# A gather, cumulative sum and projection on one core: another prologue, and GpSimd's drain moved into its own stream

## The chip, the cores and the metric

One core of a Trainium2 chip. The metric is the device time of one execution in microseconds (us); single executions of one kernel on an undisturbed chip lay within about 1% of each other. Where a ratio of two kernels is given, it is the mean time of the one's fast runs over the mean of the other's fast runs of the same rounds, so not quite the ratio of the medians that are quoted beside it. Brackets hold the 95% interval.

## The reference

```python
B, S, N, D = (16, 4096, 2048, 512)
# x [B, S, D] float32; indices [B, N] int64, sorted rows without repeats; w [D, D] float32
gathered = x[b_idx, indices, :].copy()
cs = np.cumsum(gathered, axis=1)
return np.matmul(cs, w).astype(np.float32)
```

## The kernel before

256 tiles of 128 gathered rows go through in pairs, called groups below: 128 groups. GpSimd gathers a tile (256 KB), ACT casts a pair to float16, PE sums along the rows with a triangular matrix, VectorE adds the carry, PE projects with w, ACT copies the result from PSUM, SP stores 512 KB. Every engine has a hand-written stream, in which `need(sem, n)` waits.

```python
ctx.enter_context(tc.tile_critical(no_gpsimd_drain=False))     # line 78: closes with a drain of all engines
...
def gather(t):                              # GpSimd
    g, r = divmod(t, R)                     # R = 2
    pool.need(s_c, g + 1 - NG // R)         # NG = 16: the buffer is free
    if t < FIRST:
        pool.need(s_first, 16)              # the small index load idx_first has landed
    ...
def cast(g):                                # ACT, one pair
    ...
def drain(g):                               # ACT: PSUM to an output buffer (not GpSimd's drain)
    act.need(s_o[g % NO], 16 * (g // NO))   # NO = 8 output buffers
    act.need(s_b, R * (g + 1))
    nc.scalar.copy(out=ob[g % NO][:], in_=pb[g % NB][:]).then_inc(s_e, 1)
def store(g):                               # SP
    sp.need(s_e, g + 1)
    nc.sync.dma_start(out=dst, in_=ob[g % NO][:]).then_inc(s_o[g % NO], 16)
...
# SP: idx_first, two index loads, then all of w, then the stores
# ACT:
cast(0)
act.need(s_w, 16)
nc.scalar.copy(out=w16[:], in_=w32[:]).then_inc(s_wc, 1)
for g in range(1, AH + 1):                  # AH = 2
    cast(g)
for g in range(G):
    if g + AH + 1 < G:
        cast(g + AH + 1)
    drain(g)                                # so store g follows the cast of group g + 3
```

## Time and profile before

The lines that carry the argument stand in the prediction. In short:

| kernel before, profiled run | |
|---|---|
| time | 357.12 us, median of 3 (356.56 to 357.59); the profiled run took 356.41, its span is 354.6 |
| first and last gather issued | 3.25 and 322.66 us |
| last gather landed | 337.49 us |
| first store issued, last store landed | 20.71 and 348.27 us |
| from the last store's landing to the end | 6.33 us, of which 4.97 GpSimd's drain |
| DMA share and rate, 31 to 323.6 us | 1.03, 413 GB/s |

It is to be read as a start (until DMA is full), a long middle in which DMA is full (share 1.03) and the gathers fall behind (8.6 us under way at 60 to 100 us, 15.1 at 310 to 340), a tail after the last gather, and a closing part.

### The profile page before, as it was taken

The page shows a single profiled execution, that of the slowest core. Times are in us where ns is not written, and L with a number is a line of the kernel's source. Part 1 is how long each engine was busy: PE and PEld are TensorE (multiplying, and loading weights), DVE is VectorE, ACT ScalarE, POOL GpSimd, SP SyncE. Part 2 cuts the span into 40 slices and gives each one's busy share as a digit, 9 for nine tenths or more (in the row PEclk, how much of TensorE's full clock was granted, in tenths as well). Part 3 has the DMA queues.
Part 4 walks back from the last instruction along what each step waited for, and adds up shares of the span by engine and source line. Part 5 has one row for each costly group of instructions (what it writes and reads, how often), then busy time and mean ns, then how long its engine had stood idle before and what let it go on. Part 6 is the DMA issues. An engine that isn't in the chain of part 4 may idle for free.

```text
span 354.6 us, 5833 instructions
## 1 busy us (share of the span) xinstructions
PE 301.8 (85%) x2050; PEld 149.2 (42%) x2050; DVE 178.1 (50%) x260; ACT 257.9 (73%) x258; POOL 243.7 (69%) x264
## 2 busy tenths in 40 slices
PE   0497799999899999899898988989989889898880
PEld 0253354444354444444444444444444444444440
DVE  1354465555555555555554554645555555555530
ACT  0776687787788787777777777877878778687760
POOL 6777777777777777777777777777777777774000
PEclk9999999999999999999999999999999999999995
DMA  6789999999999999999999999999999999999761
GB/s 222 224 241 384 409 410 401 415 411 418 412 417 416 415 414 415 413 416 416 415 415 414 414 413 413 411 417 415 413 417 413 416 413 414 412 415 414 293 244 74
DMA packets 40029, 135.92 MB, mean 383 GB/s; under 512 B 6465, under 2 KB 6721, under 8 KB 40001
## 3 DMA queue, kind: packets, MB, share of 16 engines
q0 software_dynamic: 20480, 67.13, 48.5%
q1 hardware_dynamic: 19520, 68.43, 47.8%
q8 instruction: 17, 0.28, 0.3%
q14 instruction: 12, 0.09, 0.1%
HBM read 68.42 MB, written 67.11 MB: 382 GB/s over the span
## 4 chain that ended last, share of the span: by engine, by line
POOL 50%; DMA 22%; issue 17%; PE 5%; ACT 3%; ACTq 0%; SPq 0%
POOL g L108 50%; DMA g<-in_x_dram,idxg 21%; PE pb L160 4%; ACT g L120 3%; PE pa L128 1%; ACT ob L172 1%; DMA idx_first<-in_indices_dram 1%; ACTq L23 0%; SPq L284 0%; SPq L78 0%
## 5 line engine op out<-in xcount | busy, mean ns | idle before, releaser
L108 POOL DMA_INDIRECT g<-in_x_dram,idxg x254 | 240.5, 947 | 77.4 <-issue 71.3
L160 PE MATMUL pb<-w,cst 128*128 128x512 f16 x1024 | 263.5, 381 | 0.0
L148 DVE TENSOR_TENSOR cst<-pa,cst 128x512 f16<-128x512 f32 x240 | 166.0, 692 | 138.1 <-PE pa L128 137.3
L120 ACT CAST g<-g 128x1024 f16<-128x1024 f32 x128 | 133.6, 1045 | 66.9 <-issue 32.2
L172 ACT COPY ob<-pb 128x1024 f32<-128x1024 f32 x128 | 129.2, 1010 | 11.4 <-PE pb L160 9.8
L128 PE MATMUL pa<-ut,g 128*128 128x128 f16 x1024 | 101.1, 222 | 38.5 <-ACT g L120 37.8
L128 PEld LDWEIGHTS pa<-ut,g 128*128 128x128 f16 x1024 | 69.4, 99 | 128.4 <-ACT g L120 97.6
L160 PEld LDWEIGHTS pb<-w,cst 128*128 128x128 f16 x1024 | 90.0, 98 | 62.0 <-issue 1.1
L143 DVE CAST cst<-pa 128x512 f16<-128x512 f32 x16 | 11.1, 692 | 20.4 <-PE pa L128 20.4
L120 ACT ACT_TABLE_LOAD x1 | 1.3, 1283 | 9.5 <-DMA g<-in_x_dram,idx_first 9.5
L229 PE MATMUL pb<-ident,idxf 128*128 128x128 f32 x2 | 0.9, 462 | 4.2 <-DVE idxf L225 4.2
L108 POOL DMA_INDIRECT g<-in_x_dram,idx_first x2 | 2.1, 1043 | 1.6 <-DMA idx_first<-in_indices_dram 1.3
L225 DVE CAST idxf<-idx 128x128 f32<-128x128 uint32 x2 | 0.5, 226 | 4.1 <-DMA idx<-in_indices_dram 4.1
L229 PEld LDWEIGHTS pb<-ident,idxf 128*128 128x128 f32 x2 | 0.4, 182 | 4.4 <-issue 4.2
L252 ACT CAST w<-w 128x2048 f16<-128x2048 f32 x1 | 1.9, 1892 | 0.0
L234 DVE CAST idxg<-pb 128x128 uint32<-128x128 f32 x2 | 0.6, 292 | 0.3
L198 POOL MEMSET ident<- 128x128 f32 x1 | 0.2, 205 | 0.5 <-SPq L78 0.5
L201 POOL TENSOR_SCALAR_AFFINE_SELECT ident<-ident 128x128 f32<-128x128 f32 x1 | 0.3, 288 | 0.1
L273 POOL MEMSET const-float32-0.0<- 128x1 f32 x1 | 0.1, 100 | 0.3 <-issue 0.3
L210 POOL TENSOR_SCALAR_AFFINE_SELECT ut<-ut 128x128 f16<-128x128 f16 x1 | 0.3, 292 | 0.0
L199 POOL MEMSET ut<- 128x128 f16 x1 | 0.2, 206 | 0.0
L273 POOL MEMSET const-uint8-127<- 128x1 uint8 x1 | 0.1, 117 | 0.0
(2 smaller groups left out, 0.2 us busy)
## 6 DMA issues: line engine op xcount, KB each, us to landing
out_dram<-ob SPq DMA_DIRECT2D x128, 512.0 KB, 7.2
g<-in_x_dram,idxg POOLq DMA_INDIRECT x254, 10.2
w<-in_w_dram SPq DMA_DIRECT2D x1, 1024.0 KB, 5.6
idx<-in_indices_dram SPq DMA_DIRECT2D x2, 128.0 KB, 2.3
g<-in_x_dram,idx_first POOLq DMA_INDIRECT x2, 5.1
idx_first<-in_indices_dram SPq DMA_DIRECT2D x1, 2.0 KB, 1.9
```

The costliest lines, as they stand in the source:

```text
L108: nc.gpsimd.indirect_dma_start(out=g32[g % (NG // R)][:, r, :], out_offset=None, in_=x_flat, in_offset=bass.IndirectOffsetOnAxis(ap=ap, ax ...
L120: nc.scalar.copy(out=g16[g % NH][:], in_=g32[g % (NG // R)][:]).then_inc(s_c, 1)
L128: mm = nc.tensor.matmul(out=pa[t % NA][:, c], lhsT=g16[g % NH][:, r, c * P : (c + 1) * P], rhs=ut[:], start=(c == 0), stop=(c == DC - 1),)
L143: nc.vector.tensor_copy(out=dst, in_=pa[t % NA][:]).then_inc(s_d, 1)
L148: nc.vector.tensor_tensor(out=dst, in0=pa[t % NA][:], in1=last.unsqueeze(2).broadcast_to([P, DC, R, Q]), op=mybir.AluOpType.add,).then_inc ...
L160: mm = nc.tensor.matmul(out=pb[g % NB][:, j], lhsT=cst[g % NC][:, c, j, :], rhs=w16[:, c, :], start=(c == 0), stop=(c == DC - 1),)
L172: nc.scalar.copy(out=ob[g % NO][:], in_=pb[g % NB][:]).then_inc(s_e, 1)
L201: nc.gpsimd.affine_select(out=ident[:], in_=ident[:], compare_op=mybir.AluOpType.is_equal, fill=0.0, base=0, pattern=[[-1, P]], channel_mu ...
L225: nc.vector.tensor_copy(out=idxf[:, k, :], in_=idx64[:, k, 0::2]).then_inc(s_if, 1)
L229: nc.tensor.transpose(out=pb[k % NB][:, 0, :P], in_=idxf[:, k, :], identity=ident[:]).then_inc(s_pt, 1)
L234: nc.vector.tensor_copy(out=idxg[:, k, :], in_=pb[k % NB][:, 0, :P]).then_inc(s_prep, 1)
L252: nc.scalar.copy(out=w16[:], in_=w32[:]).then_inc(s_wc, 1)
```

## The change

The intent: w arrives and is cast before the first gather lands (four loads on ACT's own queue, two casts on ACT, two on VectorE); ACT's function table (1.28 us, at 9.45 us in the kernel before) is loaded by a dummy activation while nothing else is there to do; dummy matmuls keep PE busy ahead of the projections, the first of which took 631 ns in the kernel before, and 379 later; the first pair is cast tile by tile; GpSimd's drain, which closed the program, goes behind its last gather.

```diff
+    zeros = const.tile([P, D], FP16)
+    spare = const.tile([P, 1], FP16)
     g32 = [const.tile([P, R, D], FP32, name=f"g32_{i}") for i in range(NG // R)]
...
-    ctx.enter_context(tc.tile_critical(no_gpsimd_drain=False))
+    ctx.enter_context(tc.tile_critical(no_gpsimd_drain=True))
...
+    def cast_first(t):
+        act.need(s_g[t], 16)
+        nc.scalar.copy(out=g16[0][:, t], in_=g32[0][:, t]).then_inc(s_c0, 1)
...
-    nc.sync.dma_start(out=w32[:], in_=w.rearrange("(c p) d -> p c d", p=P)).then_inc(s_w, 16)
...
     for t in range(T):
         gather(t)
+    nc.gpsimd.drain()
+    def busy(n):
+        pe.need(s_z, 1)
+        for _ in range(n):
+            nc.tensor.matmul(
+                out=pb[NB - 1][:, R - 1], lhsT=zeros[:, :P], rhs=zeros[:], start=True, stop=True
+            )
+    nc.vector.memset(zeros[:], 0.0).then_inc(s_z, 1)
...
+    busy(6)          # ahead of the index transposes
...
+    busy(18)         # behind them
...
+    for c in range(DC // 2, DC):
+        dve.need(s_w[c], 16)
+        nc.vector.tensor_copy(out=w16[:, c, :], in_=w32[:, c, :]).then_inc(s_wc, 1)
...
-    cast(0)
-    act.need(s_w, 16)
-    nc.scalar.copy(out=w16[:], in_=w32[:]).then_inc(s_wc, 1)
+    for c in range(DC):
+        nc.scalar.dma_start(out=w32[:, c, :], in_=w[c * P : (c + 1) * P, :]).then_inc(s_w[c], 16)
+    act.need(s_z, 1)
+    nc.scalar.copy(out=spare[:], in_=zeros[:, :1])
+    for c in range(DC // 2):
+        act.need(s_w[c], 16)
+        nc.scalar.copy(out=w16[:, c, :], in_=w32[:, c, :]).then_inc(s_wc, 1)
+    for t in range(R):
+        cast_first(t)
```

(Cut: the semaphores and the wait counts that follow from these lines.)

More of the change, by code (lines that the diff above doesn't have):

```diff
@@ L76 @@
     pb = [ps.tile([P, R, D], FP32, name=f"pb{i}") for i in range(NB)]
-    ctx.enter_context(tc.tile_critical(no_gpsimd_drain=False))
+    ctx.enter_context(tc.tile_critical(no_gpsimd_drain=True))
     def sem(name):
         return tc.alloc_semaphore(name)
-    s_first, s_w, s_ut, s_wc, s_if, s_pt, s_prep = (
-        sem(f"s_{n}") for n in ("first", "w", "ut", "wc", "if", "pt", "prep")
+    s_first, s_z, s_ut, s_wc, s_if, s_pt, s_prep, s_c0 = (
+        sem(f"s_{n}") for n in ("first", "z", "ut", "wc", "if", "pt", "prep", "c0")
     )
+    s_w = [sem(f"s_w{c}") for c in range(DC)]
     s_idx = [sem(f"s_idx{k}") for k in range(KI)]
@@ L100, in gather @@
         g, r = divmod(t, R)
-        pool.need(s_c, g + 1 - NG // R)
+        pool.need(s_c, g - NG // R)
+        if g >= NG // R:
+            pool.need(s_c0, R)
         if t < FIRST:
@@ L120, in cast @@
         nc.scalar.copy(out=g16[g % NH][:], in_=g32[g % (NG // R)][:]).then_inc(s_c, 1)
+    def cast_first(t):
+        act.need(s_g[t], 16)
+        nc.scalar.copy(out=g16[0][:, t], in_=g32[0][:, t]).then_inc(s_c0, 1)
     def sums(t):
         g, r = divmod(t, R)
-        pe.need(s_c, g + 1)
+        pe.need(s_c if g else s_c0, g or t + 1)
         pe.need(s_ut, 4)
@@ L155, in project @@
     def project(g, j):
-        pe.need(s_wc, 1)
+        pe.need(s_wc, DC)
         pe.need(s_d, R * (g + 1))
```

## The prediction

> **What bounds the kernel now.** I read the end of the run first, since an end shows what the whole run was waiting for. The chain of work that ended last, over the last 25 us (start, length, what):
>
> ```profile
> 317.66 14.81 DMA g<-in_x_dram,idxg
> 332.47 0.60 issue
> 333.07 1.05 ACT g L120
> ...
> 340.22 4.33 PE pb L160 x20
> ...
> 344.63 1.01 ACT ob L172
> ```
>
> The chain stops at 345.6 us, with the last ACT copy, but the span is 354.6 us. The missing 9 us are in the sequencers. The view of the line that opens and closes the critical section (L78: engine, operation, count, duration in ns, start in us), and the waits of the SP sequencer in the last 16 us:
>
> ```profile
> L78 POOLq DRAIN  x1: 4965/4965/4965, 348.6 to 348.6; - x1
> L78 DVEq DRAIN  x1: 17/17/17, 348.6 to 348.6; - x1
> SPq L78 <- POOLq L78: 4.8, 1, 4.8
> ```
>
> So the end is: last store issued 345.67, landed 348.3 (its issue-to-landing is the 2.6 us minimum of the stores), drains of all engines at 348.6, of which GpSimd's alone takes 4.965 us (to 353.6) while VectorE's takes 0.017, then about 1.0 us of closing barrier to 354.6. GpSimd issued its last gather at 322.7 and had been idle for 25 us when that drain started, and the last gather had landed by 337.5; the drain is not waiting for data.
>
> Next the steady state, by stretches (length, busy us and count of PE, PEld, DVE, ACT, POOL, clock, DMA share, GB/s):
>
> ```profile
> 10.00:20.00 10.00, 6.44 (x38) 3.92 (x39) 4.26 (x7) 6.85 (x7) 7.56 (x9) 1.00 0.73 212
> 20.00:31.00 11.00, 9.32 (x68) 4.71 (x67) 5.82 (x9) 8.51 (x9) 8.25 (x10) 1.00 0.93 316
> 31.00:323.60 292.60, 265.61 (x1821) 130.69 (x1820) 157.26 (x228) 226.34 (x228) 221.57 (x234) 1.00 1.03 413
> 323.60:332.00 8.40, 7.26 (x53) 3.61 (x52) 4.15 (x6) 6.09 (x7) 0.01 (x1) 1.00 0.95 385
> 332.00:337.50 5.50, 5.24 (x37) 2.55 (x35) 3.21 (x5) 4.40 (x5) 0.00 (x0) 1.00 0.59 238
> ```
>
> From 31 to 323.6 us the DMA engines are full (1.03) at 413 GB/s. GpSimd issues a gather (256 KB = 262,144 B) every 1.2525 us (0.947 busy + 0.30 issue), which asks for 209 GB/s of reads and, in the end, as much of writes: 418.6 GB/s. The demand is 1.3% above what is carried, so a backlog grows. The landing times of the gathers in the stretches 5:20, 60:100 and 310:340 us show it:
>
> ```profile
> DMA to landing us min/median/max: 3.2/3.6/4.7
> DMA to landing us min/median/max: 7.9/8.6/9.1
> DMA to landing us min/median/max: 14.8/15.1/15.3
> ```
>
> Before any store (5 to 20 us) a gather takes 3.6 us; at the end 15.1. The middle of the run is therefore bound by DMA, with GpSimd 1% behind; when GpSimd stops at 323.6, some 14 us of gathers still have to land. From the last landing (337.5) to the last store (348.3) are 10.8 us of PE, ACT and store latency.
>
> Last the start: the stretch 10 to 20 us moves 212 GB/s, half of what the DMA can, because no store exists yet. The timeline says why the first one comes at 20.7 us:
>
> ```profile
> 9.45 1.28 ACT L120 ACT_TABLE_LOAD   x1 [9.45 <-DMA g<-in_x_dram,idx_first]
> 11.70 1.89 ACT L252 CAST w<-w 128x2048 f16<-128x2048 f32 x1
> 15.69 1.04 ACT L120 CAST g<-g 128x1024 f16<-128x1024 f32 x1 [0.21 <-issue]
> 19.67 1.01 ACT L172 COPY ob<-pb 128x1024 f32<-128x1024 f32 x1 [2.93 <-PE pb L160]
> 20.71 6.90 SPq L178 DMA_DIRECT2D out_dram<-ob  x4
> ```
>
> ACT loads its table only when the first pair has landed, then casts it, then the whole of w; and after the cast at 15.69 it waits 2.93 us for PE, whose projections are slow at first. The projection's matmuls from 15 to 19 us and from 100 to 150 us (ns min/median/max):
>
> ```profile
> L160 PE MATMUL pb<-w,cst x7: 464/631/631, 16.0 to 19.0; 128*128 128x512 f16 x7
> L160 PE MATMUL pb<-w,cst x159: 379/379/379, 100.0 to 149.9; 128*128 128x512 f16 x159
> ```
>
> [...]
>
> **The change part by part.**
> *Drain.* The closing drain of GpSimd goes (4.965 us on the path) and one is put behind the last gather in GpSimd's own stream, at 323.6 us. Even if it also waits for the last landing (337.5) and then takes 4.97 us, it ends at 342.5, before the last store lands at 348.3. The other drains take 0.02 us, so the end moves by 4.965 - 0.05 = 4.9 us.
> *Table load, w casts, pair by tiles.* The dummy activation takes 1.28 us out of the first cast's path. Two of the four w casts go to DVE, idle until 12.5 us, the other two to ACT before the first gather lands. ACT loses the 1.89 us between its first and second cast. Cast 3 (gathers 6 and 7) is not earlier by this: it started 0.07 us after gather 7 landed (15.62). But cast 2 no longer queues: gather 5 landed at 13.22, so it ends near 14.3 and not 15.49.
> *Dummy matmuls.* 24 of 128x512 cost some 24 x 0.43 = 10 us cold (0.43 us: a pitch estimated from the four projections at 15.96, 1.91 us / 4 = 0.48), less once warm. Six fill the wait for the indices, 18 the wait for the first gather; ending at 10 to 12 us they may hold the first sums by 1 or 2 us, which nothing before cast 2 needs. The clock is then full when projections begin: 14.3 + sums 0.4 + projection 0.87 + sums 0.22 + projection 1.03 = 16.9 us, just after cast 3 ends (16.73).
> *First store.* The first drain can start at 16.9 and not 19.67, so the first store goes out near 18.0 and not 20.7: 2.7 us earlier.
> *w and indices.* w now goes out at about 1.0 us in four pieces beside the index load that releases GpSimd (issue 1.02, landing 2.96). [...] The index transposes shift too, but they had 0.8 us to spare before gather 2 (ready about 5.1, issue 5.94).
> *What the prologue is worth.* Between full-DMA start and end the bytes are fixed. Stores 2.7 - 0.5 = 2.2 us earlier carry (413 - 209) x 2.2 = 0.45 MB that otherwise wait; gathers 0.5 us later lose 209 x 0.5 = 0.10 MB. 0.35 MB at 413 GB/s = 0.85 us. The tail after the last landing is not touched.
> *Sum.* 4.9 + 0.85 = 5.8 us, rounded to 5.9 for the catch-up burst of stores at 20 to 26 us that should be smoother: 357.1 - 5.9 = 351.2 us.
>
> **The rivals.**
> (a) Drain cost is not removed: the remaining barrier drains GpSimd again and pays 5 us there. Against: three later GpSimd drains in this trace (the context's own, L284) take 0.03 to 0.12 us, so a second drain is cheap. Time then 356.3; chance 0.06.
> (b) The prologue gains in full, because the run is bound by the pipeline's start and not by DMA bytes: 357.1 - 4.9 - 2.7 = 349.5. Against: the DMA share of 1.03 and the growing landing times. Chance about 0.1.
> (c) The prologue gains nothing or loses: the index load is delayed by over 1.3 us behind w, or GpSimd's stream at 209 GB/s sets the end: 352.2 to 353. For: GpSimd is only 1% from the DMA's pace. Against: its stop at 323.6 leaves 14 us of backlog, so a shorter backlog does show. Chance 0.2.
> (d) The dummy matmuls end too late or the clock falls back in the gaps before cast 2: the first store gains only about 1 us, total 351.9.
>
> **Range and chances.** The drain is worth 4.9 almost surely; the prologue -0.3 to +2.2; repeated runs of before spread by 1.0 us. So 351.2, range 349.9 to 352.7. Faster by over 2% needs under 350.0, which asks for 2.2 us from the prologue, nearly rival (b): 0.12. Slower by over 2% needs a fault that I don't see.
>
> **What would show it.** Right: GpSimd's drain of about 5 us appears right after its last gather, beside other work, and about 1.3 us lie between the last store's landing and the end; the first store goes out at 17.5 to 18.5; no half-clock projections; the table load before 5 us; the last gather lands at 336 to 337. Wrong: a long GpSimd drain at the end; the first gather issued later than 4.3 us; the first store after 19.5; a last gather that lands as late as before although the first store was earlier, or earlier by the whole 2.7 us.

The sum: 4.9 for the drain and 0.85 for the prologue, together 5.8, rounded to 5.9, and so 351.2 us; but the 0.5 us that go into the 0.85 (in 2.7 - 0.5 and in 209 x 0.5) were the author's guess. What the trace of the kernel before shows: ACT's table load took 1283 ns. The first four projections, from 15.96 us, took 631 ns each, with weight loads 0.43 us apart (16.39, 16.82), which is the 0.43 of a dummy; from 19.7 us on a projection took 379 ns, and four in a row 0.86 us, 0.22 apiece. The texts call the two paces half and full clock, cold and warm; the column of the granted clock reads 1.00 in both stretches. That dummy matmuls ahead of the projections bring the faster pace was the author's estimate; no run before the change had any.

## The result, and the profile after

354.28 us, median of 6 (353.46 to 355.5), against 356.99 for the kernel before in the same rounds (356.45 to 357.88): ratio 0.9923 [0.9899, 0.9947]. So 2.7 us were saved, where 5.8 to 5.9 had been predicted.

The drain first. The kernel after, GpSimd's drain in its stream, and those of the closing part (line, engine, operation, count, ns min/median/max, first and last start):

```profile
L229 POOLq DRAIN  x1: 22219/22219/22219, 320.5 to 320.5; - x1
L312 POOLq DRAIN  x3: 34/41/135, 351.3 to 352.3; - x3
```

It ran from 320.5 to 342.7 us, that is to 2.5 us after the last gather had landed (340.20), beside other work; the drains that are left at the end are short. The prediction took the 4.965 us of the closing DRAIN for work and no wait, since it began 11 us after the last gather had landed (348.6 against 337.5; the drains of the other engines on that line took 7 to 17 ns); how much of them is work was not shown. The bar in the stream is mostly a wait for the gathers: in all nine undisturbed profiles that have this drain in the stream and the landing of the last gather, it ended 2.50 us after that landing, whether this came at 330.67 us (best_try) or at 340.22 (changed_again). From the last store's landing (350.94) to the end are now 1.66 us and not 6.33: 4.67 us gone, as predicted.

The chain of the kernel after, near its end (start, length, what), and the landing times of the gathers in 310:340 us:

```profile
321.22 16.06 DMA g<-in_x_dram,idxg
...
347.26 1.01 ACT ob L181
```
```profile
DMA to landing us min/median/max: 15.8/16.3/16.6
```

Against 345.64 before, the last copy ends at 348.27, later and not earlier. The gathers are 16.3 us under way at the end, before they were 15.1. For this pair of profiles the span splits so, by the issue and landing times of the last gather:

| profiled runs | before | after | difference |
|---|---|---|---|
| first gather issued | 3.25 | 4.30 | +1.05 |
| last gather issued | 322.66 | 323.72 | +1.06 |
| its time to landing | 14.83 | 16.48 | +1.65 |
| from there to the last store's landing | 10.78 | 10.74 | -0.04 |
| from there to the end | 6.33 | 1.66 | -4.67 |
| span | 354.6 | 352.6 | -2.0 |

So in this pair the new prologue costs 2.7 us of the span, where the prediction had it bring 0.85. The pair overstates it: this run of the kernel before was 0.6 us faster than the median, and in drain_only_3 and drain_only_4 below, which start like the kernel before, the last gather was under way for 15.71 and 15.58 us and not 14.83. By the medians the prologue costs 1.7 us (prologue_only_3). Its first store did come sooner, at 19.23 us, and the projections from 15 to 19 us take 379 ns, where those of the kernel before took 464 to 631 (kernel after):

```profile
L169 PE MATMUL pb<-w,cst x12: 379/379/379, 16.0 to 19.0; 128*128 128x512 f16 x12
```

Why the gathers start late is plain in the index load that releases them, idx_first (2 KB); kernel before, then after, issue to landing:

```profile
DMA to landing us min/median/max: 1.9/1.9/1.9
```
```profile
DMA to landing us min/median/max: 3.0/3.0/3.0
```

It is issued at 1.0 us in both. The first of the four loads of w, 256 KB each, leaves ACT at the same moment, the last at 2.4; before, w was issued behind it, at 2.49 us.

What the earlier first store came to shows in ACT's copies and casts. Kernel before, then after, in the order of time; the bracket is ACT's idle time before the instruction and what ended it:

```profile
21.84 1.01 ACT L172 COPY ob<-pb 128x1024 f32<-128x1024 f32 x1 [0.22 <-PE pb L160]
22.75 1.05 ACT L120 CAST g<-g 128x1024 f16<-128x1024 f32 x1
24.07 1.01 ACT L172 COPY ob<-pb 128x1024 f32<-128x1024 f32 x1 [0.27 <-PE pb L160]
```
```profile
23.03 1.04 ACT L125 CAST g<-g 128x1024 f16<-128x1024 f32 x1 [1.51 <-issue]
26.64 1.04 ACT L125 CAST g<-g 128x1024 f16<-128x1024 f32 x1 [1.66 <-issue]
30.18 1.04 ACT L125 CAST g<-g 128x1024 f16<-128x1024 f32 x1 [1.58 <-issue]
```

Before, the slow start had let gathered groups pile up in SBUF; from 20 to 27 us ACT and PE work them off at 2.2 us a group, and no cast waits for a gather (the next one, at 29.01 us, waits 1.76). After, nothing has piled up; each cast waits some 1.6 us for gathers that now share the DMA with the stores, and the groups come 3.5 us apart. The bracket says "issue" here, but the three casts each begin 0.07 us after the second gather of their pair had landed (22.96, 26.57 and 30.11 us). The stores' issue times (us):

| store | 0 | 1 | 2 | 3 | 4 |
|---|---|---|---|---|---|
| before | 20.71 | 22.88 | 25.10 | 27.28 | 30.99 |
| after | 19.23 | 21.54 | 25.01 | 28.62 | 32.16 |

A lead of 1.5 us at the first store is a lag of 1.2 at the fifth. The stretches of the kernel after (columns as in the prediction: the last two are DMA share and GB/s):

```profile
20.00:31.00 11.00, 7.49 (x51) 3.44 (x48) 4.47 (x7) 6.25 (x7) 8.26 (x10) 1.00 1.00 337
31.00:60.00 29.00, 26.19 (x183) 13.15 (x184) 15.41 (x23) 22.73 (x24) 21.99 (x24) 1.00 1.02 392
100.00:300.00 200.00, 180.63 (x1241) 88.96 (x1239) 107.28 (x155) 154.51 (x156) 151.22 (x161) 1.00 1.03 412
```

and two of the kernel before:

```profile
31.00:60.00 29.00, 26.03 (x183) 13.11 (x182) 15.50 (x24) 21.93 (x23) 21.99 (x24) 1.00 1.02 401
100.00:300.00 200.00, 182.29 (x1248) 89.37 (x1244) 107.88 (x156) 155.19 (x156) 151.37 (x160) 1.00 1.03 415
```

337 against 316 GB/s from 20 to 31 us (that stretch of before is in the prediction), but 392 against 401 from 31 to 60; the gain is given back. The busy share of the DMA engines does not tell their rate: 1.00 goes with 337 GB/s in the first of these stretches, 1.03 with 412 in the last. And in the middle of the run, where the same work is done, 412 against 415. From the packets' own sizes and times the two are 412.3 and 414.5: 0.5%, which over 290 us is 1.5 us. That I had not expected, and the experiments had to say whether it is chance.

### The profile page after: what moved, and what is told of

It is laid out like the page before. It is cut to its first block, busy times and chain, and to the rows that moved or that the text cites. A ratio compares the mean times of both kernels' runs of the same rounds, so it can differ in the third digit from the quotient of the medians.

```text
span 352.6 us, 5890 instructions
## 1 busy us (share of the span) xinstructions
PE 307.4 (87%) x2074; PEld 150.8 (43%) x2074; DVE 179.1 (51%) x263; ACT 257.5 (73%) x261; POOL 243.7 (69%) x264
## 3 DMA queue, kind: packets, MB, share of 16 engines
q10 hardware_dynamic: 576, 1.05, 0.8%
## 4 chain that ended last, share of the span: by engine, by line
POOL 51%; DMA 21%; issue 18%; PE 5%; ACT 3%; SPq 0%; DVE 0%; POOLq 0%; ACTq 0%
POOL g L113 51%; DMA g<-in_x_dram,idxg 20%; PE pb L169 4%; ACT g L125 2%; DMA idx<-in_indices_dram 1%; PE pa L137 1%; ACT ob L181 1%; DVE idxf L242 0%; SPq L197 0%; SPq L191 0%; POOLq L229 0%; ACTq L23 0%; DVE idxg L253 0%; SPq L312 0%; SPq L80 0%
## 5 line engine op out<-in xcount | busy, mean ns | idle before, releaser
L137 PE MATMUL pa<-ut,g 128*128 128x128 f16 x1024 | 99.7, 220 | 36.2 <-ACT g L125 34.7
L137 PEld LDWEIGHTS pa<-ut,g 128*128 128x128 f16 x1024 | 68.5, 98 | 125.4 <-ACT g L125 92.8
L235 PE MATMUL pb<-zeros 128*128 128x512 f16 x24 | 8.6, 532 | 1.5 <-DVE zeros L239 1.5
L235 PEld LDWEIGHTS pb<-zeros 128*128 128x128 f16 x24 | 3.1, 132 | 5.9 <-issue 3.5
L129 ACT CAST g<-g 128x512 f16<-128x512 f32 x2 | 1.2, 617 | 3.0 <-DMA g<-in_x_dram,idx_first 3.0
L275 ACT ACT_TABLE_LOAD x1 | 1.3, 1283 | 2.9 <-issue 2.9
L278 ACT CAST w<-w 128x512 f16<-128x512 f32 x2 | 1.2, 615 | 0.1
L256 DVE CAST w<-w 128x512 f16<-128x512 f32 x2 | 0.8, 421 | 0.0
```

The costliest lines, as they stand in the source:

```text
L129: nc.scalar.copy(out=g16[0][:, t], in_=g32[0][:, t]).then_inc(s_c0, 1)
L137: mm = nc.tensor.matmul(out=pa[t % NA][:, c], lhsT=g16[g % NH][:, r, c * P : (c + 1) * P], rhs=ut[:], start=(c == 0), stop=(c == DC - 1),)
L235: nc.tensor.matmul(out=pb[NB - 1][:, R - 1], lhsT=zeros[:, :P], rhs=zeros[:], start=True, stop=True)
L275: nc.scalar.copy(out=spare[:], in_=zeros[:, :1])
L278: nc.scalar.copy(out=w16[:, c, :], in_=w32[:, c, :]).then_inc(s_wc, 1)
```

## The experiments

The theories. **A**: the gather stream sets the end, one for one; an earlier first store is worth nothing. **B**: the prediction's: between the first store and the end DMA is full, so each us of lead of the first store is worth half a us. **C**: the two new tiles stand in front of the gather and output buffers, shift their addresses by 1056 bytes, and the DMA runs slower for it. Besides, the moved drain could disturb the last gathers.

All kernels gave the right result. Medians in us; every row has its kernel before in the same rounds:

| run | chip | time | before | ratio |
|---|---|---|---|---|
| the change, first measurement | - | 354.28 | 356.99 | 0.9923 [0.9899, 0.9947] |
| drain_only_3 | 1 | 352.56 | 357.74 | 0.9847 [0.9826, 0.9869] |
| changed_again | 9 | 353.84 | 357.04 | 0.9892 [0.9865, 0.9919] |
| w_after_idx_3 | 9 | 352.48 | 357.04 | 0.9867 [0.9841, 0.9894] |
| no_dummies_3 | 9 | 354.20 | 357.04 | 0.9912 [0.9886, 0.9939] |
| prologue_only_3 | 9 | 358.71 | 357.04 | 1.0040 [1.0013, 1.0066] |
| drain_only_4 | 12 | 352.26 | 356.99 | 0.9878 [0.9852, 0.9905] |
| tiles_last | 12 | 351.64 | 356.99 | 0.9853 [0.9830, 0.9875] |
| w_after_idx_cold | 12 | 352.97 | 356.99 | 0.9884 [0.9863, 0.9906] |
| stores_behind | 12 | 350.52 | 356.99 | 0.9828 [0.9804, 0.9853] |
| best_try | 3 | 349.67 | 356.92 | 0.9795 [0.9770, 0.9821] |

### Eight runs on disturbed chips

The first four kernels were run twice on chips on which the kernel before itself took 420 to 452 us (chip 5) and 423 to 456 us (chip 8); from 100 to 300 us the DMA moved 316 to 352 GB/s in their eight traces, in the place of 415. The traces don't show why. Single executions of one kernel lay up to 42 us apart, so nothing of a few us can be read, and none of the theories is helped or hurt by them. A ratio of fast runs could be formed for two, both unclear: no_dummies_2 1.0051 [0.9962, 1.0140] and prologue_only_2 1.0097 [0.9997, 1.0198]. Measured (medians of slow and fast executions together): drain_only 425.13 and 437.02, w_after_idx 433.37 and 450.44, no_dummies 442.97 and 437.55, prologue_only 451.69 and 438.87, against 446.52 (chip 5) and 438.31 (chip 8). Expected had been, on chip 5:

> The kernel before, with only the GpSimd drain moved behind its last gather. If the drain is worth what its bar showed (4.7 to 4.9 us), 352.2 us, 2.1 us better than the whole change; then the new prologue costs about 2 us. If instead the moved drain disturbs the last gathers (it runs from 320 to 343 us in the changed kernel), 353 to 354.5, and the prologue is worth about nothing.

> The changed kernel with the four loads of w on SP's queue behind the index loads, as before the change. Theory A (the start of the gather stream sets the end, one for one; the earlier first store is worth nothing): first gather again near 3.25 us instead of 4.30, time 1.0 us under the changed kernel, about 353.2. Theory B (my prediction's: DMA bytes from the first store on): the first store moves up 1.0 too, to about 18.2, so 352.2 or less. Theory C (the new tiles shift the buffers and the DMA runs slower): no gain, 354.3.

> The changed kernel without the 24 dummy matmuls: projections at half clock again, first store at about 20.5 to 21 us instead of 19.2. Theory A: same time as the changed kernel, 354.3, within 0.4. Theory B: the first store 1.5 us later costs about 0.75 us, 355.0.

> The changed kernel with the closing GpSimd drain put back and the one in its stream taken out. If drain and prologue add up: 357.0 + 2.0 = 359.0 us. If the moved drain is what disturbs the changed kernel, the prologue alone gives 356 to 357.

and on chip 8:

> A repeat, since the first four runs fell on a chip where the kernel before itself took 420 to 452 us, with 350 GB/s of DMA in the place of 413: no few us can be read there. Expected as before: 352.2 us if the drain is worth its bar and nothing else; 353 to 354.5 if the moved drain disturbs the last gathers.

> A repeat on another chip. Theory A (the start of the gather stream sets the end one for one): first gather near 3.25, about 353.2 us. Theory B (bytes from the first store on): 352.2 or less. Theory C (shifted buffers, slower DMA): no gain, 354.3.

> A repeat on another chip. Theory A: same as the changed kernel within 0.4 us, 354.3. Theory B: first store 1.5 us later, 355.0.

> A repeat on another chip. If drain and prologue add up: 2.0 us over the kernel before, 359.0. If the moved drain is what disturbs the changed kernel: 356 to 357.

### drain_only_3 and drain_only_4: the moved drain alone

```diff
 (kernel before)
-    ctx.enter_context(tc.tile_critical(no_gpsimd_drain=False))
+    ctx.enter_context(tc.tile_critical(no_gpsimd_drain=True))
     for t in range(T):
         gather(t)
+    nc.gpsimd.drain()
```

> A third try, because the kernel before took 420 to 456 us on both chips so far (its DMA at 350 GB/s): alone, to see whether a chip is undisturbed now. Expected on an undisturbed chip: 352.2 us if the drain is worth its bar and nothing else; 353 to 354.5 if the moved drain disturbs the last gathers.

352.56 against 357.74; again, on another chip:

> The moved drain alone, on the same chip as the three others: 5.2 us under the kernel before, about 351.9; first store near 21 to 22 us.

352.26 against 356.99. So 5.2 and 4.7 us by the medians: the drain is worth its bar, and in the stream it disturbs nothing that can be read from the times. The two lines of the change that move it bring more than the whole change did.

### changed_again and prologue_only_3: do the two halves add up?

changed_again is the kernel after, unaltered; prologue_only_3 is it with the drain put back:

```diff
 (kernel after)
-    ctx.enter_context(tc.tile_critical(no_gpsimd_drain=True))
+    ctx.enter_context(tc.tile_critical(no_gpsimd_drain=False))
-    nc.gpsimd.drain()
```

> The changed kernel once more, beside the others on the same chip: 354.3 us if the first measurement holds; 352 if its loss of 2 us against the moved drain alone was that day's chip.

> Third try. The moved drain alone brought 352.56 against 357.74. If drain and prologue add up, this is about 2 us over the kernel before, 359 to 360; if the two only disturb each other, 357 to 358.

353.84 and 358.71, same chip: 4.87 us apart, and the closing drain of prologue_only_3 is back at its old length (its line):

```profile
L80 POOLq DRAIN  x1: 4965/4965/4965, 350.8 to 350.8; - x1
```

The prologue alone is slower than the kernel before, by 1.7 us of the medians (0.4% [0.1, 0.7]). 358.71 lies between the two expectations, 359 to 360 and 357 to 358, so it is the 4.87 us on one chip, the drain's bar again, that decides: the halves add up, and the loss is the prologue's.

### w_after_idx_3: w behind the index loads

```diff
 (kernel after)
+    for c in range(DC):                      # on SP, behind the index loads
+        nc.sync.dma_start(out=w32[:, c, :], in_=w[c * P : (c + 1) * P, :]).then_inc(s_w[c], 16)
-    for c in range(DC):                      # on ACT, in front
-        nc.scalar.dma_start(out=w32[:, c, :], in_=w[c * P : (c + 1) * P, :]).then_inc(s_w[c], 16)
```

> Third try on what is now an undisturbed chip. Theory A (the start of the gather stream sets the end one for one): first gather near 3.25, 1.0 us under the changed kernel, about 353.2. Theory B (bytes from the first store on): 352.2 or less. Theory C (shifted buffers, slower DMA): no gain, 354.3.

352.48, 1.36 us under changed_again on the same chip. idx_first lands after 1.9 us again, the first gather is issued at 3.16 and not 4.34, the first store at 17.97 and not 19.26: the 18.0 that the prediction had named. Theory C as it was put (no gain) falls; the late start costs about what it is late. A and B (352.2 or less) can't be told apart by the time alone. But the stores' issue times speak against B: 17.97, 20.46, 24.13, 28.74, 32.38. In drain_only_4 they are 22.67, 24.84, 27.06, 29.24, 31.46: the first 4.7 us later, the fifth 0.9 us earlier, and the two kernels are equally fast (0.9867 and 0.9878), where B would have the first 2.3 us faster (4.7 x 204 / 413); the 0.9 us that theory C may cost it, below, would cover less than half of that. Nor are the bytes there that B counts on. Over the first 60 us the DMA moved 325 GB/s in w_after_idx_3 and 323 in drain_only_4, so 0.12 MB more; 4.7 us at B's 204 GB/s would be 0.96 MB. w_after_idx_cold and tiles_last (below), with first stores near 20 us, moved 328. These are single profiles: drain_only_3 moved 319, and the same kernel 321 and 310 in after and changed_again.

### no_dummies_3: without the dummy matmuls

```diff
 (kernel after)
-    busy(6)
+    busy(0)
-    busy(18)
+    busy(0)
```

> Third try. Theory A: same as the changed kernel within 0.4 us, 354.3. Theory B: first store 1.5 us later, 355.0.

354.20, 0.36 us over changed_again, with the first store at 21.57 and not 19.26. B wanted some 1.1 us for 2.3 us of store; and the first gather of its profiled run was 0.2 us later, too. By the medians the dummy matmuls are worth 0.2 to 0.4 us; the runs overlap (353.37 to 354.67 and 352.75 to 354.33), so the time alone excludes neither nothing nor B's 1.1.

They don't hold the pace for good, either. In changed_again the granted clock was 0.53 from 29.4 to 33.0 us (stretch, columns as before, the third number from the end), and the four projections at 29.68 took 1.91 us and not 1.03; the casts were waiting for gathers, and PE had stood idle for 2.51 us just before:

```profile
29.40:33.00 3.60, 3.60 (x16) 1.79 (x17) 1.38 (x2) 1.84 (x2) 2.69 (x4) 0.53 0.98 353
```

### w_after_idx_cold and tiles_last: the first store, and the addresses

w_after_idx_cold is w_after_idx_3 without the dummies (the edit of no_dummies_3). tiles_last is w_after_idx_3 with the new tiles behind all others:

```diff
 (w_after_idx_3)
-    zeros = const.tile([P, D], FP16)
-    spare = const.tile([P, 1], FP16)
     g32 = [...]
     ...
     ob = [...]
+    zeros = const.tile([P, D], FP16)
+    spare = const.tile([P, 1], FP16)
```

With them in front, the first gather buffer lies 1056 bytes further on in every partition (built, the program has it at byte 34752 and not 33696); with them last, all old buffers have their old addresses.

> The kernel with w behind the index loads, without the dummy matmuls: gathers start at 3.2 as there, but the first store comes at about 20.5 instead of 18.0. Theory B (my prediction's: an earlier first store is worth half its lead in DMA bytes): 1.2 us over that kernel, 353.6. Theory A (the first store is worth nothing, the gather stream all): the same within 0.3, 352.4.

> The kernel with w behind the index loads, and the two new tiles allocated after all others, so that every old buffer has its old address (from the traces: 100 to 300 us carries 315.5 units of 256 KB in the two kernels with the old addresses, 313.7 to 314.9 in the five with the new ones, some 0.3%). Theory C (the shifted addresses cost DMA rate): 1.0 us less than with the tiles in front, and so about 0.5 under the moved drain alone, 351.4. If the addresses don't matter: 0.4 to 0.6 over the moved drain alone, 352.4.

352.97 and 351.64 on the same chip. By chance the two have nearly the same first store in their profiled runs, 20.02 and 19.89 us, and the same first gather, 3.20 and 3.15: in tiles_last PE was slow from 12.99 to 18.6 us. Eight sums took 1.03 us and not 0.61 as in w_after_idx_3, four projections 1.91 and not 1.03. Before that PE had stood idle for 0.59, 1.02 and 1.41 us, with 0.40 us of sums between; that this is the cause was not shown (PE's instructions of tiles_last; the bracket is idle time):

```profile
11.19 0.40 PE L137 MATMUL pa<-ut,g 128*128 128x128 f16 x4 [1.02 <-ACT g L129]
12.99 1.03 PE L137 MATMUL pa<-ut,g 128*128 128x128 f16 x8 [1.41 <-ACT g L125]
14.77 1.91 PE L169 MATMUL pb<-w,cst 128*128 128x512 f16 x4
```

So here two kernels with the same start of gathers and of stores in their profiled runs differ by 1.33 us by the medians, and what is left between them are the 24 dummies, worth 0.2 to 0.4 in no_dummies_3, and the addresses. (When the other executions, which were not profiled, sent their first stores is not known; and of the 1.9 us between the two profiled spans, 1.2 are the last store, which took 3.84 us to land in w_after_idx_cold and 2.64 in tiles_last.)

The rates of the middle, from the packets, GB/s over 100 to 300 us: old addresses 414.5 (before), 414.7 and 414.6 (drain_only_3, drain_only_4), 414.2 (tiles_last); new addresses 412.3 (after), 413.8 (changed_again), 413.3 (w_after_idx_3), 413.1 (w_after_idx_cold), 413.0 (no_dummies_3), 413.4 (prologue_only_3). The groups don't overlap; the means are 414.5 and 413.2, 0.3%, which is 0.9 us of a middle of 290. stores_behind and best_try below, with old addresses, moved 410.8 and 410.4; they hold stores back during this stretch and so can't be compared. C is thus supported in size and sign, but thinly: after and changed_again are the same kernel and lie 1.5 apart, more than the two means, and only tiles_last has the new prologue at the old addresses. It is not proved: a kernel that adds the two tiles to the kernel before and nothing else was not run, and by the ratios to the kernel before tiles_last (0.9853) and w_after_idx_3 (0.9867, another chip) overlap.

B wanted 1.2 us between w_after_idx_cold and w_after_idx_3. By the ratios, 0.9884 and 0.9867, it is 0.6 us, on different chips and within the intervals of 0.8 us and more. This run alone does not decide between A and B.

Without its two faults the new prologue is worth 351.64 against 352.26 for the moved drain alone: 0.6 us, with overlapping runs (351.32 to 352.05 and 351.47 to 353.68).

### stores_behind: what does the end hang on?

If the end hangs on the last gather, and gathers and stores share a full DMA, then stores that are put off let the gathers through. SP lets them fall up to four groups behind, in four steps over the run, and lets all go when four groups are left:

```diff
 (drain_only)
-    NO = 8
+    NO = 14
...
-        sp.need(s_e, g + 1)
+        behind = max(0, min(4, (g - 8) // 24))
+        sp.need(s_e, max(g + 1, min(g + 1 + behind, G - 4)))
```

> The moved drain alone, and SP lets the stores fall up to four groups behind, in four steps over the run (14 output buffers for 8), and lets them go once four groups are left. If the end hangs on the last gather, and the gathers share a full DMA with the stores, four stores of 512 KB put off give the gathers 4 x 1.24 us: last gather at about 333.5 instead of 338, time 347.5 to 348.5. If the stores put off come back as a tail of their own, or if the gathers' pace is not set by the stores, 351 to 353.

350.52, 1.74 us under drain_only_4 on the same chip. The landing time of the gathers in 310:340 us, and two stretches:

```profile
DMA to landing us min/median/max: 10.0/10.6/11.1
```
```profile
330.00:334.00 4.00, 3.63 (x26) 1.67 (x23) 2.22 (x4) 2.65 (x3) 0.00 (x0) 1.00 0.64 260
334.00:338.00 4.00, 3.62 (x24) 1.93 (x24) 1.38 (x2) 2.27 (x3) 0.00 (x0) 1.00 1.03 407
```

The last gather landed at 333.24 and not 337.72: 4.5 us sooner, near the 4 x 1.24 expected (an estimate: 512 KB at the 413 GB/s of the kernel before), and the last store was issued 4.5 us sooner (341.33). It landed only at 347.08, though, because the stores put off stood in front of it, while from 330 to 334 the DMA had been let run at 260 GB/s. So the mechanism is right, and the second line of the expectation also came true in part: of 4.5 us some 3 came back as a tail.

### best_try: the pieces together

```diff
 (tiles_last)
-    NO = 8
+    NO = 16
...
-        sp.need(s_e, g + 1)
+        behind = max(0, min(5, (g - 8) // 20))
+        sp.need(s_e, max(g + 1, min(g + 1 + behind, G - 5)))
```

> The best pieces together: the new prologue with w behind the index loads and the new tiles last, the moved drain, and stores up to five groups behind (16 output buffers), let go once the fifth-last group is drained. The four-group version had the last gather at 333.2 and not 337.7, but the stores put off left the DMA a hole of some 1.5 us at 330 to 334 and a tail of 5.7 us for the last store. With the release one group sooner and one group more put off: last gather at 331 to 333, last store landed by 345.5 to 346.5, time 348 to 349.5. If the stores put off only move the wait to the end: 350 to 351, no better than the four-group version.

349.67 against 356.92: the lowest time of all, 2% under the kernel before (0.9795 [0.9770, 0.9821], so at the 2% mark unclear). Against stores_behind (0.9828 [0.9804, 0.9853], another chip) the intervals overlap. The gathers of 310:340 us land after 8.0 us, and the hole is closed:

```profile
DMA to landing us min/median/max: 7.9/8.0/8.4
```
```profile
330.00:334.00 4.00, 3.84 (x27) 1.96 (x26) 2.54 (x4) 2.23 (x3) 0.00 (x0) 1.00 1.03 417
334.00:338.00 4.00, 3.63 (x17) 1.47 (x15) 0.04 (x1) 2.30 (x3) 0.00 (x0) 1.00 1.03 417
```

The last gather landed at 330.67, the last store was issued at 338.76 and landed at 345.71, 7 us later: the end now hangs on the stores themselves. The time is just above the 348 to 349.5 that were expected.

## Why the prediction was wrong

By its own steps:

- **The drain, 4.9 us: right.** 4.87 us (prologue_only_3 against changed_again), 4.7 and 5.2 (drain_only). In the stream it waits for the last landing, as allowed for, and ends 2.5 us after it and not 4.97. Rival (a), a second long drain, did not happen.
- **Table load, w casts, dummies, first store at 18.0 less the delay: right.** 17.97 in w_after_idx_3; 19.23 in the kernel after, where the gathers start 1.05 us late. That the projections took 379 ns in both is in part luck: in tiles_last four of them took 1.91 us and not 1.03 (first store 19.89), as rival (d) feared. Two sums are loose and change nothing: 1.91 / 4 is 0.48 and not the 0.43 us of a dummy, which is the distance of the weight loads, and the sum to 16.9 gives 16.8.
- **The 0.5 us of delay for the index load: mis-sized.** That w goes out beside it was seen, but the 0.5 was a guess; it measured 1.05 us of issue, and putting w behind the indices gave back 1.36 us of time. This term alone made the prologue's sum about nothing: with 1.5 us of lead and 1.05 of delay the prediction's own formula gives (204 x 1.5 - 209 x 1.05) / 413 = 0.2 us of gain.
- **"What the prologue is worth": the step that failed.** It took DMA to be full at 413 GB/s from the first store on, so that each us of lead brings 204 KB that stay brought. By that step the prologue gains 0.2 us even with the measured delay; prologue_only_3 lost 1.7. The trace shows a start-up of another kind: 337 GB/s from 20 to 31 us at a share of 1.00; after an early first store the groups come 3.5 us apart, because each cast waits for gathers that now have stores beside them; after a late one the groups that have piled up go at 2.2 us apart. By the fifth store the early kernels have no lead left (w_after_idx_3 against drain_only_4: 4.7 us earlier, then 0.9 later). Of the 0.96 MB that this lead should bring, 0.12 are there by 60 us. So the first store's time is no measure of bytes. One of the prediction's own signs of being wrong came true with it: the last gather landed no sooner (340.20 against 337.49 us) although the first store was earlier.
- **What no step had: the DMA rate of the middle,** 0.3% lower in the mean of the six profiles with the new tiles in front, about 0.9 us. That the addresses are its cause is supported by tiles_last, not proved.

The terms, from the medians: drain -4.9; w in front of the indices +1.4; and so, by subtraction from what was measured twice (-2.7 and -3.2), about +0.8 and +0.3 for the rest of the prologue, addresses among it. The causes of this rest stay open. Rival (c), "the prologue gains nothing or loses", named the right place, but for one of three causes, and it was given 0.2; its 353 us was still too low.

## What to carry to other kernels

A cost that shows as one bar on the closing path, and that can be done beside other work, is worth counting at its full length; here two lines brought 4.7 to 5.2 us for a bar of 4.97. A prologue that keeps engines busier is worth only what it moves on the stream that sets the end: look first at whether anything new goes out beside the small load which that stream waits for (here it landed after 3.0 us and not 1.9), and check a few steps into the steady state whether the lead is still there (here 4.7 us at the first store, none at the fifth). Where two streams share a full DMA and the end hangs on one of them, try to hold the other back, and release it before the first runs dry: here that brought 1.74 us (stores_behind against drain_only_4), with the DMA down at 260 GB/s from 330 to 334 us; with the release a group sooner and one group more put off (best_try) it moved 417 there.
